# S5 layer with a top-4 mixture of experts on one core: another router order, S5 rotations on GpSimd, sums kept in PSUM, a ring of eleven pairs

## The chip, the core and the metric

The kernel runs on one core of a Trainium2 chip. The metric is the device time in microseconds (us) of one execution, from the first to the last instruction with what lies around them; lower is better. All data is float32.

## What is computed

One decoder layer for 256 tokens of width 1024 (the reference, cut to what the kernel does):

```python
proj = x @ w_in                                  # 1024 x (768 + 256)
y_mix = s5_mixer(proj[..., :768], ...)           # 48 groups x 64 complex states, scan over 256 tokens, gelu, gate
y_mem = memory_cross_attention(proj[..., 768:], mem_k, mem_v)   # 4 heads over 256 memory rows
y = concatenate([y_mix, y_mem]) @ w_out
h = layer_norm(ALPHA * x + y, ln1_g, ln1_b)
logits = h @ router_w + router_b                 # 32 experts
top_val, top_idx = top_k(logits, 4); gates = softmax(top_val)
gu = h[rows of expert e] @ w_gu[e] + b_gu[e]     # 1024 x 2048
a = clamped_swiglu(gu); y_e = a @ w_down[e] + b_down[e]         # 1024 x 1024
out = layer_norm(ALPHA * h + sum over experts of gate * y_e, ln2_g, ln2_b)
```

The weights of the 32 experts are 12.6 MB each and are all read, 403 MB of the 424.62 MB that the program moves.

## The kernel before

**Memory.** One SBUF tile `big` is cut into slots of 8 KB per partition (1 MB), 22 of them. A slot holds several tensors one after another; the table `slot_of` (L85 to L92) says which ("wsc" after "ptmp0" in slot 0, and so on). For the experts' weights the slots 0 to 19 are taken two at a time as blocks of 2 MB: `ring` (L99) lists ten pairs in the order in which they come free, and `next_block` (L101) takes the next one in rotation. An expert takes six blocks: four of `w_gu` (`load_gu`, L1128) and two of `w_down` (`load_down`, L1137). All these loads are issued by SP in program order; a load waits until its pair's last reader is done, and the next load waits behind it. At expert 18 one pair leaves the ring for constants of the end.

**Order.** `Ordered` (L127) and `pin` (L116) keep VectorE (V), ScalarE (S), SP and TensorE (through `mm` and `tr`, L141 to L145) in program order. GpSimd (G) isn't pinned, and VectorE isn't from L1165 on. PSUM has eight banks of 128x512, handed out by `bank` (L105) from one pool; a new bank waits for the release of an old one.

**S5 and attention (L157 to L882).** The projection runs on TensorE; the discretised S5 parameters and their powers `apw` are made by VectorE (L310 to L424). `power` (L467) multiplies the matrices B and C with the powers, 128x2048 at a time, on VectorE, and GpSimd adds the halves. `kb` (L553) makes the kernel taps `kr`, VectorE adds D (`dsk`) at L563, `kc` (L614) transposes them. Then VectorE makes the rotations' table `w_re`, `w_im` (L568 to L608, L662): three squarings `sq` of the angle (24 columns each), and `doubled`, which doubles the table from 1 to 32 columns; each complex product is six instructions (`cmul4`, L576). `rotated` (L729) applies them to the transposed state `sv`, scans it, and the output products `yb` follow. ScalarE in between copies `kc`, shifts, and copies transposes (`m1tp`, `sip`, `stp`).

**Gate and router.** After the memory half of W_out (`out_mem`, `yp`), TensorE transposes the gate's bias and gamma/beta (`bgp`, L856 to L861), makes the router's bias with beta folded in (`rbp`, L865) and multiplies the gate's weights (`zp`, L871). W_out's other 24 products (512 columns each) go into four banks `yp` (L930 to L937), one per token tile i and column half hf; VectorE adds the residual and takes the statistics of LayerNorm (L938, L939), GpSimd makes the reciprocal root. VectorE normalises x2 at once (L943) and GpSimd applies gamma and beta (`affine`, L917). `logits` (L964) transposes the normalised x2 of a tile (`hTp`), multiplies it with gamma-scaled router weights `wg` into 32 rows, copies, and `logits_t` turns them back; `chosen` (L984) takes the top 4 and a mask, `ranks` (L996) counts each token's place in its expert.

**Experts (L1250 to L1322).** `gather` (L1031) makes one-hot matrices `oh` and multiplies them with h (`xgp`): the tokens of two experts at once, 64 slots each. Per expert: `up` (L1064, banks `gu`), `act` (L1075, clamp and SwiGLU on VectorE and ScalarE), `act_t` (transposes `atp`), `up_bias` for the next expert, `down` (L1095, bank `dn`). After each pair `combine` (L1109) multiplies with the gates' transposes (`ogT`) into four banks `cb`, and VectorE adds them to `acc` in SBUF. At expert 30 `acc` is loaded into four banks `accp` by products with the identity, and the last sums go on there; `finish` (L1208) normalises and stores.

## Time and profile before

| | |
|---|---|
| runs | 1080.88, 1082.1, 1080.85 us; median 1080.88 |
| the profiled execution | 1082.37 us, its span 1080.7 us |
| TensorE (PE) busy | 1004.5 us, 93% of the span |
| VectorE (DVE), ScalarE (ACT), GpSimd (POOL) busy | 276.5, 152.1, 45.2 us |
| moved | 424.62 MB, mean 393 GB/s |
| TensorE's granted clock, mean | 0.994 of full speed |

The page of the profile divides the span into 40 equal slices and gives, for each, the busy tenths of every engine and the rate of the transfers. A group of instructions is named by line, engine, operation and tiles (out<-in); "L135" and "L142" are the lines of helpers, so groups are told apart by their tiles. TensorE's records come in passes: x16 for eight products. "Idle before <-releaser" is how long the engine stood before the instruction and what ended that.

### The profile page before, as it was taken

The numbers are of one execution on the slowest core, as the hardware profiler recorded it, in microseconds if no ns is written. First come the engines' busy times: TensorE is split into PE (matmuls) and PEld (weight loads), VectorE is DVE, ScalarE is ACT, GpSimd is POOL, SyncE is SP. The second block draws the span as 40 slices with busy tenths as digits, with TensorE's granted clock in tenths as the row PEclk, the third lists the DMA queues.
The fourth block names the chain that finished last, engine by engine and source line by source line (L and its number), as shares of the span: only waits on it lengthen the run. The fifth ranks groups of instructions, "written<-read, shape, count | busy, mean of one in ns | idle before, by whom it ended". The sixth has DMA issues, their size and how long they took to land.

```text
span 1080.7 us, 12435 instructions
## 1 busy us (share of the span) xinstructions
PE 1004.5 (93%) x5301; PEld 440.3 (41%) x5301; DVE 276.5 (26%) x627; ACT 152.1 (14%) x286; POOL 45.2 (4%) x57
## 2 busy tenths in 40 slices
PE   9998999999999999898989888899989999898994
PEld 8885554434343433243333232333433342323331
DVE  7993251121212221112121112102121211121013
ACT  3493020101010100010101010000101110100001
POOL 1800030000000000000000000000000000000001
PEclk9999999999999999999999999999999999999998
DMA  9959779999999999999999999999999999999992
GB/s 300 157 180 343 306 270 425 426 428 426 427 426 426 426 429 427 425 426 428 426 426 427 427 410 428 426 426 427 427 426 426 427 427 426 428 427 427 426 422 102
DMA packets 43843, 424.62 MB, mean 393 GB/s; under 512 B 11218, under 2 KB 14182, under 8 KB 19080
## 3 DMA queue, kind: packets, MB, share of 16 engines
q1 hardware_dynamic: 43288, 422.73, 95.3%
q10 hardware_dynamic: 496, 1.05, 0.3%
q8 instruction: 43, 0.70, 0.3%
q14 instruction: 16, 0.13, 0.0%
HBM read 421.93 MB, written 1.84 MB: 392 GB/s over the span
## 4 chain that ended last, share of the span: by engine, by line
DMA 53%; PE 37%; DVE 8%; issue 1%; ACT 0%; ACTq 0%; POOL 0%; DVEq 0%; SPq 0%
DMA big<-in_exp_w_gu_dram 46%; PE gu_e L142 14%; PE dn_e L142 7%; DMA big<-in_exp_w_down_dram 7%; DVE big L135 5%; PE xgp_e L142 3%; PE tail L142 3%; PE yp L142 3%; PE cb_e L142 2%; PE zp L142 1%; PE accp L142 1%; PE atp_e L145 1%; PE busy L142 1%; PE lgp L142 0%; PE yb L142 0%
## 5 line engine op out<-in xcount | busy, mean ns | idle before, releaser
L142 PE MATMUL gu_e<-big,xg_e 128*64 128x512 f32 x1984 | 442.9, 595 | 54.7 <-DMA big<-in_exp_w_gu_dram 54.0
L142 PEld LDWEIGHTS gu_e<-big,xg_e 128*64 128x64 f32 x1984 | 137.1, 137 | 354.6 <-issue 247.6
L142 PE MATMUL dn_e<-big,xl_te 128*64 128x512 f32 x960 | 212.6, 595 | 0.0
L1078 DVE TENSOR_SCALAR xl_e<-gu_e 128x512 f32<-128x512 f32 x31 | 21.4, 692 | 443.1 <-PE gu_e L142 443.1
L142 PEld LDWEIGHTS dn_e<-big,xl_te 128*64 128x64 f32 x960 | 66.3, 137 | 144.3 <-issue 119.9
L1105 DVE COPY y_e<-dn_e 64x512 f32<-64x512 f32 x30 | 20.5, 683 | 234.7 <-PE dn_e L142 234.7
L135 ACT ACTIVATE gu_e<-xl_e 128x512 f32<-128x512 f32 x31 | 18.6, 601 | 416.4 <-DVE xl_e L1078 416.4
L142 PE MATMUL xgp_e<-oh_e,big 128*128 128x128 f32 (+1 forms) x544 | 67.1, 282 | 0.0
L142 PEld LDWEIGHTS xgp_e<-oh_e,big 128*128 128x128 f32 x544 | 65.5, 196 | 0.1
L142 PE MATMUL cb_e<-y_e,ogT_e 128*128 128x512 f32 x112 | 52.1, 603 | 0.0
L135 ACT COPY y_e<-dn_e 64x512 f32<-64x512 f32 x30 | 17.4, 581 | 243.8 <-DVE y_e L1105 243.8
L148 DVE TENSOR_TENSOR big<-big,cb_e 128x512 f32<-128x512 f32 x52 | 33.5, 679 | 6.2 <-PE cb_e L142 6.1
L142 PE MATMUL gu_e<-bgu,ident 32*64 32x512 f32 x248 | 33.7, 612 | 0.0
L142 PEld LDWEIGHTS cb_e<-y_e,ogT_e 128*128 128x128 f32 x112 | 20.2, 189 | 30.3 <-issue 24.3
L135 DVE TENSOR_TENSOR big<-big 128x768 f32<-128x768 f32 (+10 forms) x35 | 25.4, 740 | 14.6 <-ACT big L135 14.1
L142 PE MATMUL yp<-big 128*128 128x512 f32 x64 | 28.2, 595 | 0.0
L135 DVE TENSOR_TENSOR big<-big,tab 128x2048 f32<-128x2048 f32 x12 | 26.6, 2276 | 0.2 <-DVE big L135 0.2
L148 POOL TENSOR_TENSOR big<-big 128x512 f32<-128x512 f32 (+1 forms) x10 | 26.1, 2632 | 2.7 <-DVE big L135 1.9
L135 ACT COPY xg_e<-xgp_e 128x512 f32<-128x512 f32 x32 | 18.7, 585 | 48.3 <-PE xgp_e L142 48.3
L135 ACT COPY xl_te<-atp_e 128x512 f32<-128x512 f32 x30 | 17.6, 585 | 52.7 <-PE atp_e L145 46.0
L1080 DVE TENSOR_SCALAR xr_e<-gu_e 128x512 f32<-128x512 f32 x31 | 21.4, 691 | 2.9 <-PE gu_e L142 0.2
L1081 DVE SCALAR_TENSOR_TENSOR xr_e<-xr_e,xl_e 128x512 f32<-128x512 f32 x32 | 22.0, 688 | 0.5
(282 smaller groups left out, 578.3 us busy)
## 6 DMA issues: line engine op xcount, KB each, us to landing
big<-in_exp_w_gu_dram SPq DMA_DIRECT2D x128, 2048.0 KB, 38.1
big<-in_exp_w_down_dram SPq DMA_DIRECT2D x62, 2048.0 KB, 39.1
big<-in_l_w_in_dram SPq DMA_DIRECT2D x3, 1024.0 KB
big<-in_w_out_dram SPq DMA_DIRECT2D x3, 1024.0 KB
big<-in_exp_w_down_dram SPq DMA_DIRECT2D x3, 1024.0 KB
big<-in_x_dram SPq DMA_DIRECT2D x3, 512.0 KB
big<-in_l_s_w_glu_dram SPq DMA_DIRECT2D x2, 768.0 KB
big<-in_l_w_in_dram SPq DMA_DIRECT2D x2, 512.0 KB
```

Of the source, the lines that this page charges most:

```text
L135: return lambda *a, **k: pin(f(*a, **k))
L142: pin(PE.matmul(o, lhsT, rhs, start=start, stop=stop, skip_group_check=shared))
L145: pin(PE.transpose(o, in_, ident if idn is None else idn))
L148: return (eng or V).tensor_tensor(out=o, in0=x0, in1=x1, op=op)
L1078: V.tensor_scalar(out=xl_, in0=ps[0], scalar1=7.0, scalar2=None, op0=ALU.min)
L1080: V.tensor_scalar(out=xr, in0=ps[1], scalar1=7.0, scalar2=-7.0, op0=ALU.min, op1=ALU.max)
L1081: V.scalar_tensor_tensor(out=xr, in0=xr, scalar=1.0, in1=xl_, op0=ALU.add, op1=ALU.mult)
L1105: eng(y[:, 512 * dh : 512 * dh + 512], ps[dh][64 * dh : 64 * dh + 64, :])
```

## The change

- `big` gets a 23rd slot, the ring an eleventh pair; tensors change their slots, and the pairs' order is new. `apw`, its scratch and `r8` move into a slot. `bgu` is held as four quarters of 512 columns, in four loads.
- S5: the three squarings, the first four columns of the table (`w4`) and the squares up to the fourth power's are made on GpSimd right after `r8`; VectorE doubles from 4 on. D is added by three TensorE products into the banks of `kb`.
- The transposes of biases and gamma/beta and the folded router bias (now spread to all partitions) are made after the first `kps`, copied by ScalarE; `wg` on GpSimd earlier; the column sums of `wg` give a correction `lfix`.
- Router: logits come from x2 before normalisation, token by row, and are corrected with mean and reciprocal root (`fixed`); h is made by VectorE in two steps (`first`, `second`), and the order of the stages is written out.
- Experts: `combine` sums into four banks `accp` from the first pair on; `gather_pair` fills its banks one after the other and comes before the gates' transposes; `y` has one buffer.

```diff
...
-NBIG = 22
+NBIG = 23
...
-        "mem_sb tz1 gb", "wk wgl1", "x_sb m1p1 wgl2", "xT prob yT", "rawb m1p2 wo0", "rawc m1p0 wo1", "win_2 wo3",
-        "win_3 wgl0", "win_0 sv wo2", "win_1 tz2 ymT", "wv h_sb", "ut kr pT x2 acc",
+        "mem_sb tz1 gb", "ut kr pT x2", "x_sb m1p1 wgl2", "xT prob", "rawb m1p2 wo0", "rawc m1p0 wo1", "win_2 wo3",
+        "win_3 wgl0", "win_0 sv wo2", "win_1 tz2 ymT", "wk wgl1", "pow yT", "wv h_sb",
...
-    ring = [2 * k + n for k in (0, 1, 2, 3, 4, 6, 8, 7, 9, 5) for n in range(0, 2, ROWS)]
+    ring = [2 * k + n for k in (0, 1, 2, 3, 4, 8, 6, 10, 7, 9, 5) for n in range(0, 2, ROWS)]
...
-    bgu = keep_t("bgu", (2 * NE, D))
-    for b in range(2):
-        SP.dma_start(bgu[NE * b : NE * b + NE, :], b_gu[0, :, D * b : D * b + D])
+    bgu = keep_t("bgu", (P, 512))
+    for q in range(4):
+        SP.dma_start(bgu[NE * q : NE * q + NE, :], b_gu[0, :, 512 * q : 512 * q + 512])
...
-    apw = small("apw", (P, 2, Q + 1, NG))
-    t1, t2 = small("t1", (P, 4, NG)), small("t2", (P, 4, NG))
+    pw = big_tile("pow")
+    apw = pw[:, 0:864].rearrange("p (q k g) -> p q k g", q=2, g=NG)
+    t1, t2 = (pw[:, 864 + 192 * n : 1056 + 192 * n].rearrange("p (k g) -> p k g", g=NG) for n in range(2))
...
     for _ in range(3):
         tt(mv_, mv_, mv_, ALU.mult, G)
-    r8 = small("r8", (P, 24, NC))
+    r8 = pw[:, 1248:2016].rearrange("p (r c) -> p r c", c=NC)
     G.tensor_copy(r8, mv_.unsqueeze(2).to_broadcast([P, 24, NC]))
     G.memset(r8[:, :, 0], 0.0)
+
+    def cmul4(o_re, o_im, x_re, x_im, y_re, y_im, t, eng=None):
+        yield tt(t[0], x_re, y_re, ALU.mult, eng)
+        yield tt(t[1], x_im, y_im, ALU.mult, eng)
+        yield tt(t[2], x_re, y_im, ALU.mult, eng)
+        yield tt(t[3], x_im, y_re, ALU.mult, eng)
+        yield tt(o_re, t[0], t[1], ALU.subtract, eng)
+        yield tt(o_im, t[2], t[3], ALU.add, eng)
+
+    def sq(o, i_, t, eng=None):
+        return cmul4(o[:, 0], o[:, 1], i_[:, 0], i_[:, 1], i_[:, 0], i_[:, 1], t, eng)
+
+    e_, f_, w4, s4g = small("e_", (P, 2, 24)), small("f_", (P, 2, 24)), small("w4", (P, 2, 24, 4)), small("s4g", (P, 4, 24, 2))
+    s4q = [s4g[:, n, :, 0] for n in range(4)]
+    G.memset(w4[:, 0, :, 0], 1.0)
+    G.memset(w4[:, 1, :, 0], 0.0)
+    for o, i_ in ((e_, cv), (f_, e_), (e_, f_)):
+        together(sq(o, i_, s4q, G))
+    G.tensor_copy(w4[:, :, :, 1], e_)
+    together(sq(f_, e_, s4q, G))
+    together(cmul4(
+        w4[:, 0, :, 2:4], w4[:, 1, :, 2:4], w4[:, 0, :, 0:2], w4[:, 1, :, 0:2],
+        *(f_[:, q].unsqueeze(2).to_broadcast([P, 24, 2]) for q in range(2)), [s4g[:, n] for n in range(4)], G,
+    ))
+    together(sq(e_, f_, s4q, G))
 
     tab = [bank("tab0")[:, 0 : (Q + 1) * NG], bank("tab1")[:, 0 : (Q + 1) * NG]]
     S.copy(tab[0], apw[:, 0].rearrange("p k g -> p (k g)"))
@@ -559,8 +585,9 @@
                     ps[32 * j : 32 * j + 32, P * l : P * l + P], ca_pad[:, NH * g : NH * g + 2 * NH], m1p[g],
                     l == 0, True, True,
...
-    tt(kr[:, :, NH : 2 * NH], kr[:, :, NH : 2 * NH], dsk, ALU.add)
+        pv_ = ps.rearrange("p (l n) -> p l n", l=4)
+        mm(pv_[:, :, 0:NH], ident, dsk[:, 4 * b : 4 * b + 4, :], False, True, True)
+        S.copy(kr[:, 4 * b : 4 * b + 4, NH:144], pv_)
...
+    for q, w_ in enumerate((wre, wim)):
+        G.tensor_copy(w_[:, :, 0:4], w4[:, q])
...
-    for o, i_ in ((e_, cv), (f_, e_), (e_, f_)):
-        together(sq(o, i_))
-    G.memset(wre[:, :, 0], 1.0)
-    G.memset(wim[:, :, 0], 0.0)
-    w_state = [1, e_, f_]
+    w_state = [4, e_, f_]
...
+                    wre[:, :, n : 2 * n], wim[:, :, n : 2 * n], *((w4[:, 0], w4[:, 1]) if n == 4 else (wre[:, :, 0:n], wim[:, :, 0:n])),
+                    b_[0], b_[1], [u[:, :, 0:n] for u in us],
                 ),
-                sq(nxt, cur) if 2 * n < NC else iter(()),
+                sq(nxt, cur, s4) if 2 * n < NC else iter(()),
...
+    bgp = bank("bgp")
+    tr(bgp[:, 0:6], bg6, ident[0:6, 0:6])
+    tr(bgp[:, 8:24], gl16, ident[0:16, 0:16])
+    bglu, gcol = small("bglu", (P, 6)), small("gcol", (P, 16))
+    S.copy(gcol, bgp[:, 8:24])
+    S.copy(bglu, bgp[:, 0:6])
+    wg, wgs, lfix = keep_t("wg", (P, KT, NE)), small("wgs", (P, NE)), keep_t("lfix", (P, 2, NE))
+    rbp = bank("rbp")
+    for kt in range(KT):
+        mm(rbp[:, 0:NE], gcol[:, KT + kt : KT + kt + 1].to_broadcast([P, P]), wr[:, kt, :], kt == 0, False)
+    mm(rbp[:, 0:NE], ones[0:1, :], rb, False, True)
+    S.copy(lfix[:, 1], rbp[:, 0:NE])
...
+    tt(wg, wr, gcol[:, 0:KT].unsqueeze(2).to_broadcast([P, KT, NE]), ALU.mult, G)
...
-    bgp = bank("bgp")
...
-    tt(wg, wr, gcol[:, 0:KT].unsqueeze(2).to_broadcast([P, KT, NE]), ALU.mult, G)
-    rbp = bank("rbp")
-    for kt in range(KT):
-        mm(rbp[0:1, 0:NE], gcol[:, KT + kt : KT + kt + 1], wr[:, kt, :], kt == 0, False)
-    mm(rbp[0:1, 0:NE], ones[0:1, 0:1], rb, False, True)
-    V.tensor_copy(rb2, rbp[0:1, 0:NE])
+    V.tensor_reduce(out=wgs, in_=wg.rearrange("p k e -> p e k"), axis=AX.X, op=ALU.add)
...
+    wsp = bank("wsp")
+    mm(wsp[:, 0:NE], ones, wgs, True, True)
+    S.mul(lfix[:, 0], wsp[:, 0:NE], -1.0)
...
-        n = 2 if tag in ("ogT", "y") else 1
+        n = 2 if tag == "ogT" else 1
...
+    mean, rs = [None] * 2, [None] * 2
+    lgp = bank("lgp")
+
+    def added(i, hf):
+
+        hs = slice(512 * hf, 512 * hf + 512)
+        out_q(i, hf, range(QO, 8))
+        stt(x2[:, i, hs], x2[:, i, hs], ALPHA, yp[i][hf], ALU.mult, ALU.add)
+        norm_stats(x2[:, i, hs], hf, f"{i}")
+
+    def turned(i, hf):
+        ps = bank(f"hTp{i}{hf}")
+        for k in range(4):
+            kt = 4 * hf + k
+            tr(ps[:, P * k : P * k + P], x2[:, i, kt * P : (kt + 1) * P])
+        S.copy(hT[i][:, 4 * hf : 4 * hf + 4, :], ps.rearrange("p (k n) -> p k n", k=4))
+
+    def logits(i, hf):
+        for kt in range(4 * hf, 4 * hf + 4):
+            mm(lgp[:, NE * i : NE * i + NE], hT[i][:, kt, :], wg[:, kt, :], kt == 0, kt == KT - 1, True)
+
+    def normed(i):
+        mean[i], rs[i] = norm_of_stats(f"{i}")
+
+    def first(i, hf):
+        hs = slice(512 * hf, 512 * hf + 512)
+        stt(h_sb[:, i, hs], x2[:, i, hs], mean[i], gb[:, 0, hs], ALU.subtract, ALU.mult)
+
+    def second(i, hf):
+        hs = slice(512 * hf, 512 * hf + 512)
+        stt(h_sb[:, i, hs], h_sb[:, i, hs], rs[i], gb[:, 1, hs], ALU.mult, ALU.add)
+
+    def fixed(i):
+
+        stt(lg[:, i, :], lfix[:, 0], mean[i], lgp[:, NE * i : NE * i + NE], ALU.mult, ALU.add)
+        stt(lg[:, i, :], lg[:, i, :], rs[i], lfix[:, 1], ALU.mult, ALU.add)
+
+    def chosen(i):
...
-                    ps[b][64 * hf : 64 * hf + 64, :], sel[b],
-                    bgu[NE * b : NE * b + NE, 512 * hf : 512 * hf + 512], True, False, True,
+                    ps[b][64 * hf : 64 * hf + 64, :], sel[2 * b + hf],
+                    bgu[NE * (2 * b + hf) : NE * (2 * b + hf) + NE, :], True, False, True,
...
+    added(0, 0)
+    added(0, 1)
+    turned(0, 0)
+    normed(0)
+    first(0, 0)
+    first(0, 1)
+    added(1, 0)
+    turned(0, 1)
+    logits(0, 0)
+    logits(0, 1)
+    fixed(0)
+    second(0, 0)
+    chosen(0)
+    second(0, 1)
+    rkp0, rkp1 = bank("rkp0"), bank("rkp1")
+    added(1, 1)
+    turned(1, 0)
+    mm(rkp0[:, 0:NE], lower, msk[:, 0, :], True, True)
+    turned(1, 1)
+    normed(1)
+    ranks(0, rkp0[:, 0:NE])
+    logits(1, 0)
+    logits(1, 1)
+    mm(rkp1[:, 0:NE], ones, msk[:, 0, :], True, False, True)
     ps = up_bias("e0", sel_of(0))
-    lg0 = logits_t(0, lg0)
-    lg1 = logits(1)
...
-    lg1 = logits_t(1, lg1)
-    mm(rkp1[:, 0:NE], ones, msk[:, 0, :], True, False, True)
+    oh_e0 = wt((P, 2, 2 * CAP), "oh", "e0")
+    ts(oh_e0[:, 0, 0:CAP], iota64, rk[:, 0, 0:1], ALU.is_equal)
+    first(1, 0)
+    first(1, 1)
+    fixed(1)
+    chosen(1)
...
+    def gather_pair(n, xg, ranks):
+
+        oh = wt((P, 2, 2 * CAP), "oh", n)
+        for i in range(2):
+            for k, rank in enumerate(ranks):
+                ts(oh[:, i, CAP * k : CAP * k + CAP], iota64, rank[i], ALU.is_equal)
+        for k4 in range(2):
+            ps = bank(f"xgp{k4}_{n}")
+            for i in range(2):
+                for kt in range(4 * k4, 4 * k4 + 4):
+                    mm(
+                        ps[:, P * (kt % 4) : P * (kt % 4) + P], hv[:, i, kt // ROWS, kt % ROWS], oh[:, i, :],
+                        kt % 4 == 0 and i == 0, i == 1, True,
+                    )
+            S.copy(xg[:, 4 * k4 : 4 * k4 + 4, :], ps.rearrange("p (k c) -> p k c", k=4))
...
+    accp = []
+
+    def combine(y, ogT, late=None, stop=False):
+
+        if not accp:
+            alpha_id = wt((P, P), "xl", "alpha")
+            V.tensor_scalar(out=alpha_id, in0=ident, scalar1=ALPHA, scalar2=None, op0=ALU.mult)
+            for i in range(2):
+                accp.append([bank(f"accp{i}{hf}") for hf in range(2)])
+                for hf in range(2):
+                    mm(accp[i][hf], alpha_id, h_sb[:, i, 512 * hf : 512 * hf + 512], True, False)
+        for i in range(2):
+            for dh in range(2):
+                ds_ = slice(512 * dh, 512 * dh + 512)
+                mm(accp[i][dh], ogT[:, i, :], y[:, ds_], False, stop)
+                if late is not None:
+                    mm(accp[i][dh], late[:, D + P * i : D + P * i + P], late[:, ds_], False, False)
+
+    def combine_on(n, y, ogT, acc):
         for i in range(2):
             for dh in range(2):
                 ps = bank(f"cb{i}{dh}_{n}")
                 ds_ = slice(512 * dh, 512 * dh + 512)
-                mm(ps, ogT[:, i, :], y[:, ds_], True, late is None)
-                if late is not None:
-                    mm(ps, late[:, D + P * i : D + P * i + P], late[:, ds_], False, True)
-                if first:
-                    a = stt(acc[:, i, ds_], h_sb[:, i, ds_], ALPHA, ps, ALU.mult, ALU.add)
-                else:
-                    a = tt(acc[:, i, ds_], acc[:, i, ds_], ps, ALU.add)
-                last_of["acc"] = a.ins.name
+                mm(ps, ogT[:, i, :], y[:, ds_], True, True)
+                tt(acc[:, i, ds_], acc[:, i, ds_], ps, ALU.add)
...
     def rest_of_ranks():
-        chosen(1, lg1)
         mm(rkp1[:, 0:NE], lower, msk[:, 1, :], False, True, True)
+        second(1, 0)
         ranks(1, rkp1[:, 0:NE])
-        busy(3)
+        busy(2)
 
     xgs = wt((P, KT, 2 * CAP), "xg", "e0")
-    gather("e0", xgs[:, :, 0:CAP], [ranks_of(0)], iota64, rest_of_ranks)
-    V = nc.vector
+    gather("e0", xgs[:, :, 0:CAP], [ranks_of(0)], iota64, rest_of_ranks, lambda: second(1, 1), oh_e0)
...
+    V = nc.vector
...
-            accp = [[bank(f"accp{i}{hf}") for hf in range(2)] for i in range(2)]
             a = act(f"e{e}", ps)
+            combine(*last)
             y = wt((P, D), "y", f"e{e}")
-            for i in range(2):
-                for hf in range(2):
-                    ds_ = slice(512 * hf, 512 * hf + 512)
-                    mm(accp[i][hf], ident, acc[:, i, ds_], True, False)
-                    mm(accp[i][hf], last[2][:, i, :], last[1][:, ds_], False, False)
...
-        if e % 2 == 0:
-            y = wt((P, D), "y", f"e{e}")
         if last is not None:
             combine(*last, late if e == NE - 12 else None)
             last = None
+        if e % 2 == 0:
+            y = wt((P, D), "y", f"e{e}")
         if e % 2:
+            xgs = wt((P, KT, 2 * CAP), "xg", f"e{e + 1}")
+            gather_pair(f"e{e + 1}", xgs, [ranks_of(e + 1), ranks_of(e + 2)])
             ogT = gates_t(f"e{e}", og, P)
             og = wt((P, 2, 2 * CAP), "og", f"e{e + 1}")
-            xgs = wt((P, KT, 2 * CAP), "xg", f"e{e + 1}")
-            gather(f"e{e + 1}", xgs, [ranks_of(e + 1), ranks_of(e + 2)], iota64)
...
+    slot_of["acc"] = ring.pop(0)
+    acc = big_tile("acc").rearrange("p (i d) -> p i d", i=2)
...
```

## Rows read from the trace of the kernel before

**Rows 1.** The page's second part, bytes moved in 40 equal slices of the span.

```profile
GB/s 300 157 180 343 306 270 425 426 428 426 427 426 426 426 429 427 425 426 428 426 426 427 427 410 428 426 426 427 427 426 426 427 427 426 428 427 427 426 422 102
```

**Rows 2.** TensorE timeline, 500-565 us: start, us, engine line op out<-in xcount [idle <-releaser].

```profile
512.32 3.65 PE L142 MATMUL gu_e<-big,xg_e 128*64 128x512 f32 x16 [1.25 <-DMA big<-in_exp_w_gu_dram]
517.22 3.65 PE L142 MATMUL gu_e<-big,xg_e 128*64 128x512 f32 x16 [1.25 <-DMA big<-in_exp_w_gu_dram]
```

**Rows 3.** Chain of waits, `up` of experts 1 and 3: start us, us, what.

```profile
181.18 13.73 PE gu_e L142 x64
...
233.42 13.73 PE gu_e L142 x64
```

**Rows 4.** Timeline of TensorE, 117 to 156 us (router, first gather, first `up`).

```profile
139.92 1.04 PE L145 MATMUL hTp<-ident,big 128*128 128x128 f32 x8
...
148.88 2.08 PE L142 MATMUL xgp_e<-oh_e,big 128*128 128x64 f32 x16
...
154.55 1.94 PE L142 MATMUL gu_e<-big,xg_e 128*64 128x512 f32 x8 [0.68 <-ACT xg_e L135]
```

**Rows 5.** Chain of waits, from the last `up` with a wait to the tail.

```profile
1021.89 3.65 PE gu_e L142 x16
1025.54 7.06 PE accp L142 x16
...
1048.35 7.04 PE tail L142 x32
```

**Rows 6.** Timeline of SP's queue, 122 to 170 us (issues of expert weights).

```profile
138.40 10.29 SPq L135 DMA_DIRECT2D big<-in_exp_w_gu_dram  x3
...
158.25 3.76 SPq L135 DMA_DIRECT2D big<-in_exp_w_down_dram  x2
```

**Rows 7.** Windows of 3 us: length, busy (x) by engine, PEclk, DMA share, GB/s.

```profile
135.00:138.00 3.00, 3.00 (x8) 1.33 (x7) 2.29 (x5) 0.00 (x0) 2.10 (x3) 1.00 0.00 0
159.00:162.00 3.00, 3.00 (x18) 1.00 (x16) 0.00 (x0) 0.00 (x0) 0.00 (x0) 1.00 0.98 295
```

**Rows 8.** Timeline of VectorE, 14 to 59 us (sine series, first squaring).

```profile
14.90 0.44 DVE L135 SCALAR_TENSOR_TENSOR sn<-sn,r 128x48 f32<-128x48 f32 x2
...
57.99 0.45 DVE L135 TENSOR_TENSOR s<-cv 128x24 f32<-128x24 f32 x4
```

**Rows 9.** Timeline of ScalarE, 49 to 75 us.

```profile
52.16 2.50 ACT L135 COPY big<-kc 128x256 f32<-128x256 f32 x6 [2.40 <-PE kc L145]
...
69.86 1.83 ACT L135 COPY big<-stp 128x512 f32<-128x512 f32 x4
```

**Rows 10.** Chain of waits, 71 to 140 us.

```profile
71.84 1.70 DVE big L135 x2
...
98.20 3.44 PE yp L142 x8
...
103.40 15.89 PE zp L142 x96
119.29 20.80 PE yp L142 x48
```

**Rows 11.** Timeline of TensorE, 42 to 60 us.

```profile
51.41 2.84 PE L145 MATMUL kc<-ident,big 128*128 128x128 f32 x24 [2.06 <-DVE big L135]
```

**Rows 12.** Timeline of GpSimd, 12 to 40 us.

```profile
14.99 0.83 POOL L148 TENSOR_TENSOR mv__402<-mv__402 128x24 f32<-128x24 f32 x3
...
30.30 0.59 POOL L148 TENSOR_TENSOR dsk<-dsk,same 128x192 f32<-128x192 f32 x1 [12.48 <-DMA dsk<-in_l_s_d_dram]
```

**Rows 13.** Timeline of VectorE, 139 to 152 us (router of the second token tile).

```profile
140.12 0.69 DVE L135 SCALAR_TENSOR_TENSOR big<-big,yp 128x512 f32<-128x512 f32 x1 [2.02 <-PE yp L142]
...
145.12 1.01 DVE L148 TENSOR_TENSOR ex<-m 128x4 f32<-128x4 f32 x1
...
148.96 0.20 DVE L135 MAX8 m<-lg 128x8 f32<-128x32 f32 x1
...
150.02 0.37 DVE L135 TENSOR_REDUCE msk<-xr_og 128x32 f32<-128x128 f32 x1
```

More of the change, by code (lines that the diff above doesn't have):

```diff
@@ L1039, in gather @@
             for k, rank in enumerate(ranks):
-                ts(oh[:, i, CAP * k : CAP * k + CAP], base, rank[i], ALU.is_equal)
+                if i or first_too:
+                    ts(oh[:, i, CAP * k : CAP * k + CAP], base, rank[i], ALU.is_equal)
+            if i:
+                after()
             for kt in range(KT):
@@ L1322 @@
         if e % 2:
-            last = (f"e{e}", y, ogT)
+            last = (y, ogT)
     finish(
```

98 lines of the change are left out of this document (13 added, 85 removed).

## Prediction

> **What bounds the kernel now.** I read the page's slices first. From the seventh of the 40 on, the core moves 425 to 429 GB/s in nearly every slice; the first six hold 157 to 343 [rows 1]. So the time is the moment from which the weight stream never stops, plus the bytes then left, plus a tail; what matters is what delays that moment.
>
> The timeline of TensorE in mid-stream shows who waits: each block of gate and up weights (2 MB) makes TensorE stand 1.25 us, and the blocks come 4.90 us apart [rows 2]. An expert is six blocks, 29.4 us of transfer. In the early experts TensorE has the data and needs 52.24 us from one `up` to the second after it, 26.1 us per expert [rows 3]. From the first `up` to the end of expert 30's the mean is (1025.54 - 13.73 - 154.55) / 30 = 28.6 us [rows 3, 4, 5], so TensorE has about 2.5 us per expert to lose before it is the bound.
>
> Then SP's issues and the three-microsecond windows. Ten blocks fit the ring before expert 0 is consumed. Blocks 8 to 10 go out from 138.40 us, when W_out's last products release their slots; block 11 goes out at 158.25 us, 3.70 us after `up` of expert 0 began and had used up the first block [rows 4, 6]. Between 135 and 138 us nothing moves, and between 159 and 162 us only 295 of some 425 GB/s, so block 11 flows from 159.9 us, 1.65 us after its issue [rows 7]. From there the stream is whole: block 12 starts at 159.9 + 4.9 = 164.8 us.
>
> **The S5 stage.** Forty-two small complex-product instructions leave VectorE (three squarings, the doublings from 1 and 2 with their squarings); at 0.45 / 4 = 0.11 us [rows 8] that is 4.6 us, and the add of D, some 0.5 us, goes too. I cost this gain at nothing: the rotations need S5's transposed state, whose ScalarE copies end at 69.86 + 1.83 = 71.69 us, and the first rotation starts at 71.84 us [rows 9, 10]. ScalarE is busy in one run back to the `kc` copies at 52.16 us, so VectorE will only arrive early and stand.
>
> What sets the stage is when `kc` starts. Today TensorE ends `kps` at 49.35 us and waits 2.06 us for VectorE's add of D [rows 11]. That wait goes, but new work stands in its place: three products with D at 0.26 us (2.08 / 8, the gather's 128x128 by 64 [rows 4]) ahead of `kps`, then two transposes at 0.13 us (1.04 / 8 [rows 4]), a small ScalarE copy of some 0.4 us with its handovers, and nine router products, whose stationary operand is now 128 columns wide, again at 0.26 us. That makes 49.35 + 0.8 + 0.3 + 0.4 + 2.3 = 53.1 us, 1.7 us later than 51.41 us. After the 0.15 us that the rotations had in hand, **plus 1.5 us**. Below, the nine cost a transpose's 0.13 us each: plus 0.4. A gain is excluded, since no operation before `kc` gets shorter. Above, GpSimd holds VectorE back somewhat: plus 3.5, half of the rival below. I take 0.26, the row with the same width of stationary operand.
>
> GpSimd gets 36 of those products between its last preparation and 30.30 us, where it stood idle for 12.48 us; at 0.83 / 3 = 0.28 us they fill 10 us of it [rows 12]. Behind them on its queue are the multiplication for D and the sums of the first matrices, which TensorE needs at 43 us; by these prices they start as before. Where the gap is too short, what is late next is `kb`. SP's queue gets two issues more, the bias table in four loads instead of two, ahead of the load of `wv`, which is read some 40 us later: nothing.
>
> A page of the Trainium skill speaks against this part: SBUF — State Buffer, section "SBUF: two separate sides", says that VectorE and GpSimd share one port pair under an exclusive lock, so a VectorE instruction with two SBUF inputs blocks for the whole of a GpSimd one. One row fits it: a four-element product took 1.01 us beside a GpSimd product, where one of 24 elements takes 0.11 us alone [rows 8, 13]. By that rule alone the sum would come out as the second rival's.
>
> **From the gate to the first expert.** The transposes of the biases, the folded router bias and their copies leave the gap between `yp` and `zp`: 103.40 - (98.20 + 3.44) = 1.76 us [rows 10]. One product of ones with the weight sums comes before `yp` instead, 0.3 us with its start: **minus 1.5**, within 0.2.
>
> In the router I walked the new order from the first `yp` on (119.29 us now, 35.3 us ahead of the first `up` at 154.55 us [rows 4, 10]). The 24 products take 20.8 us as now, but four half-transposes of token tile 0 (0.52 us each pair of four, two such) and eight logit products (0.26 us) stand inside them, 3.1 us, so the last quarter is summed at 23.9. VectorE adds and takes statistics: 0.69 + 0.69 + 0.21 + 0.15 with gaps, 2.0 [rows 13]: 25.9. Then rank, one-hot, two halves of `first` at 0.7: 27.7. Two corrections of the logits at 0.2: 28.2. Top-4 and mask as now from 148.96 to 150.39 us, 1.4 [rows 13]: 29.6. The count product queues behind the first half of the gather, which TensorE ends at about 30.8, and with rank and one-hot that gives 31.7. The second half of the gather 2.08 and the copy 0.7 [rows 4]: 34.5. **Minus 0.8**; with the last halves of `second` uncovered plus 1, with logit products at 0.13 us minus 2.
>
> So `up` of expert 0 starts at 154.55 + 1.5 - 1.5 - 0.8 = 153.75 us.
>
> **The eleventh pair.** Blocks 6 to 8 can go at the end of the gate, 9 and 10 when the last W_out products end (22 to 24 us after the first, about 141 and 143 us), 11 when `second` of the last quarter ends (32.4 after it, about 151.7 us). They land by 158.1 us. Block 12 needs expert 0's first block to be used: 153.75 + 3.70 + 1.65 = 159.1 us. Against 164.8 us that is 5.7 us, of which 0.8 is counted above: **minus 4.9**. Bounds: minus 4.9 and nothing.
>
> **The experts.** The sum in four PSUM banks takes 52 VectorE adds away, which TensorE doesn't wait for: nothing. The gather of a pair now precedes the gates' transposes; the same work, and ScalarE's copy of the activations comes some 0.4 us later in odd experts. At expert 2, TensorE waits about 2 us for a scaled identity, which takes the buffer of the activation and so stands behind it on VectorE (the first sum and the activation's transposes queue behind that wait), and does four more products, 3.5 us by half of the tail's eight [rows 5]. Slack covers both: nothing. Without it they would cost 0.2 us per expert and 5.5 us once.
>
> **The tail.** Four products that reload the sum are gone, half of 7.06 us [rows 5]. But the last block of expert 30's down weights lands six blocks after 1021.89 us, at 1051.3 us; half of `down`, 3.5 us, follows, to 1054.8, where now it ends at 1055.39 [rows 5]. **Minus 0.5**; bounds minus 3 and nothing.
>
> Sum: -0.8 - 4.9 - 0.5 = -6.2 us. The profiled execution took 1082.37 us (its span 1080.7 and 1.7 around it), so 1076.2; it stands 1.5 us above the median of the three runs, 1080.88, which gives **1074.7 us**. All starts shift alike, so sizes within the head only move this number.
>
> **The rivals.** First, the eleventh pair buys nothing: its block is released so late, by `second` or by the queue in front of it on SP, that block 12 starts no sooner than by the earlier `up`. For it: the slots with gamma and x2 are the last released. Against: 158.1 is before 159.1. Then 1079.6 us. Chance 0.11.
>
> Second, GpSimd blocks VectorE in the S5 preparation. From 30.30 - 12.48 = 17.82 us on [rows 12] VectorE has some 27 products of two SBUF operands before the big ones with the power tables; if each waits for one GpSimd product of 0.28 us, 7.5 us come before everything: 1082.2 us. For it the 1.01 us row [rows 13]; against it, beside three GpSimd products at 14.99 us [rows 12] two steps of VectorE's sine series took 0.44 us together [rows 8], not a GpSimd product more each. Chance 0.08.
>
> Third, the slower side: with four banks left, `up`, gather, gate and activation transposes, the next bias products and `down` wait for each other's evictions. The point that decides is 2.5 us per expert. At 3.0 us an expert takes 29.1 us, 30 times 0.5 above today's mean, 16 us, less 0.8 and less the 3.5 us of the tail: 1093 us. Against it: an eviction takes 1.83 / 4 = 0.46 us on ScalarE [rows 9], and five of them in a row are 2.3 us. Chance 0.06.
>
> Fourth, better: router products at 0.13 us and the tail's 3.5 us partly kept; S5 plus 0.4, router minus 1.5, tail minus 1.5: minus 8.9 us, 1072 us. Chance 0.17. My forecast has 0.58.
>
> **How the numbers follow.** A measurement here can tell 0.2%, 2.2 us, from no change. Forecast (its own range 1071.5 to 1078) and fourth rival are faster, 0.75; the first and the larger part of the second lie within it, 0.17; the third and the rest are slower, 0.08. The range from 1070.5 to 1080.5 takes in the bounds of the S5 stage, the router and the tail, and the first rival.
>
> **What would show it.** Right: `kc` about 1.7 us later, the rotations waiting for ScalarE, `up` of expert 0 near 153.8 us, block 12 issued near 157.5 us, a dead stretch of the queue still ahead of W_out's end, and VectorE idle in the experts. Wrong: full GB/s from the same time as before (first rival), VectorE's products after 17.8 us stretched (second), TensorE waiting for ACT or DVE between `up` and `down` by over 2.5 us (third).

## The result, and the profile after

The changed kernel takes 1072.99 us (median of ten executions, 1071.89 to 1079.34); the kernel before took 1080.89 us (median of ten). The ratio of the means is 0.994, with a 95% interval of 0.9928 to 0.9953; by the medians it is faster by 7.9 us, where 6.2 us were forecast. Seven of ten executions lie between 1071.9 and 1073.5 us, three near 1079 us with a lower mean granted clock of TensorE (0.987 instead of 0.995); the experiments come back to these.

The page of the profiled execution (1072.42 us, span 1070.6 us) shows where the stream of weights begins to be whole; against [rows 1] the fifth and sixth slices hold 424 and 314 GB/s instead of 306 and 270:

```profile
GB/s 303 166 151 329 424 314 429 428 417 430 427 428 427 425 429 428 426 430 427 428 426 429 429 409 428 429 428 427 427 427 428 427 428 427 427 428 428 429 422 98
```

TensorE's timeline, with the columns of [rows 4], gives the milestones of the head: `kb`, with which the S5 stage begins (the products with D, second row, stand between its parts), the router's bias ahead of `kc`, the transposes `stp` of S5's state, the products `yb` that wait for the scan, the gate's sum of weights, the first `yp` behind it, the two halves of the first gather, and `up` of expert 0; further down the scaled identity and the tail.

```profile
41.91 1.32 PE L142 MATMUL kb<-big 128*32 128x128 f32 x32
43.16 0.43 PE L142 MATMUL kb<-dsk,ident 128*128 128x64 f32 x2
...
50.40 1.97 PE L142 MATMUL rbp<-wr,gcol 128*128 128x32 f32 x16 [0.31 <-ACT gcol L135]
...
52.63 2.84 PE L145 MATMUL kc<-ident,big 128*128 128x128 f32 x24
...
70.40 1.84 PE L145 MATMUL stp<-ident,big 128*128 128x128 f32 x12
...
88.04 0.42 PE L142 MATMUL yb<-big 128*32 128x128 f32 x8 [0.97 <-DVE big L135]
88.91 2.61 PE L142 MATMUL yb<-big 128*32 128x128 f32 x88 [0.44 <-DVE big L135]
...
115.95 0.41 PE L142 MATMUL wsp<-wgs,ones 128*128 128x32 f32 x2
116.19 13.98 PE L142 MATMUL yp<-big 128*128 128x512 f32 x32
...
144.11 2.10 PE L142 MATMUL xgp_e<-oh_e,big 128*128 128x64 f32 x16
...
146.97 2.10 PE L142 MATMUL xgp_e<-oh_e,big 128*128 128x64 f32 x16
149.80 7.52 PE L142 MATMUL gu_e<-big,xg_e 128*64 128x512 f32 x34 [0.73 <-ACT xg_e L135]
...
219.04 5.40 PE L142 MATMUL accp<-big,xl_alpha 128*128 128x512 f32 x8 [2.45 <-DVE xl_alpha L1163]
...
1042.06 3.65 PE L142 MATMUL tail<-big 128*64 128x512 f32 x16 [1.14 <-DMA big<-in_exp_w_down_dram]
```

VectorE's timeline: the powers in S5's preparation, the big products behind them, the first rotation, and the mask of the second token tile. GpSimd's, below it, holds some of what moved there, and the last row is ScalarE's, the four copies of the transposed state.

```profile
17.86 5.19 DVE L135 TENSOR_TENSOR big<-big 128x48 f32<-128x48 f32 x18
...
26.26 4.49 DVE L135 TENSOR_TENSOR big<-big,tab 128x2048 f32<-128x2048 f32 x2 [0.19 <-DVE big L135]
...
72.02 2.88 DVE L135 TENSOR_TENSOR big<-big 128x768 f32<-128x768 f32 x3 [4.15 <-PE stp L145]
...
144.94 0.37 DVE L135 TENSOR_REDUCE msk<-xr_og 128x32 f32<-128x128 f32 x1
```

```profile
17.27 0.80 POOL L148 TENSOR_TENSOR s4g<-cv 128x24 f32<-128x24 f32 x4
...
23.10 1.17 POOL L148 TENSOR_TENSOR f__414<-s4g 128x24 f32<-128x24 f32 x2
...
27.88 0.45 POOL L148 TENSOR_TENSOR e__413<-s4g 128x24 f32<-128x24 f32 x2
```

```profile
71.09 1.83 ACT L135 COPY big<-stp 128x512 f32<-128x512 f32 x4
```

SP's queue, to hold against [rows 6]: block 11 is the first of the two at 147.64 us, ahead of `up`, and block 12 the second, 153.5 us, 3.7 us after `up` began.

```profile
147.64 6.18 SPq L135 DMA_DIRECT2D big<-in_exp_w_down_dram  x2
```

And its windows of 3 us, as in [rows 7]: the stretch without transfers ahead of W_out's end is still there, the dent behind the first `up` is small.

```profile
135.00:138.00 3.00, 3.00 (x16) 2.04 (x16) 2.02 (x7) 0.10 (x1) 0.00 (x0) 1.00 0.03 11
...
153.00:156.00 3.00, 3.00 (x18) 1.00 (x14) 0.99 (x5) 0.00 (x0) 0.00 (x0) 1.00 0.97 371
```

**Reading the two profiles together.** Three stretches are compared, from milestones of the timelines: `kb` to the first rotation (the S5 stage), rotation to the first `up`, first `up` to the end of the span. What lies ahead of `kb` is the arrival of x and W_in; it moved by up to 7 us between executions (41.9 to 49.2 us) and is no part of the change. All kernels of the study stand here, each by its profiled execution:

| kernel | `kb` to rotation | rotation to `up` | `up` to end |
|---|---|---|---|
| before | 28.97 | 82.71 | 926.15 |
| after | 30.11 | 77.78 | 920.8 |
| e1_again, e9_after_there (after) | 31.51, 31.57 | 77.79, 77.80 | 921.15, 921.02 |
| e2_ten_pairs | 31.70 | 77.78 | 926.21 |
| e3_alpha_late | 29.86 | 77.78 | 920.54 |
| e4_rot_dve | 29.87 | 77.79 | 920.44 |
| e5_alpha_twice | 31.53 | 82.02 | 924.97 |
| e6_rbp_gate | 26.91 | 80.78 | 920.23 |
| e7_sbuf_sum | 29.86 | 77.79 | 925.67 |
| e8, e11 (late gap, twice) | 27.25, 27.71 | 78.33, 78.30 | 920.10, 920.61 |
| e10_gap_only | 27.71 | 78.31 | 919.78 |
| e12_small_more | 27.25 | 87.67 | 919.97 |

Between the profiled executions of before and after, the span fell by 10.1 us: 0.96 by the earlier arrival (`kb` at 42.87 and 41.91 us), plus 1.14 in S5, minus 4.93 to the first `up`, minus 5.35 from there on. Part of the 4.93 was the bad luck of one execution: before, TensorE stood 1.85 us ahead of `yb`, and its granted clock fell to the lower level for these products, 4.28 us instead of 2.61 us. The timeline (with `stp`, which is wanted further down) and the windows (TensorE's columns alone) of before:

```profile
69.17 1.84 PE L145 MATMUL stp<-ident,big 128*128 128x128 f32 x12
...
87.67 0.43 PE L142 MATMUL yb<-big 128*32 128x128 f32 x8 [1.85 <-DVE big L135]
88.54 4.28 PE L142 MATMUL yb<-big 128*32 128x128 f32 x88 [0.44 <-DVE big L135]
```

```profile
90.00:92.00 2.00, 2.00 (x44) 0.50 0.89 287
```

Without that and the arrival, the two profiles differ by 7.5 us, near the medians' 7.9.

### The profile page after: what moved, and what is told of

Read it like the earlier page. It is cut to its first block, busy times and chain, and to the rows that moved or that the text cites. A ratio compares the mean times of both kernels' runs of the same rounds, so it can differ in the third digit from the quotient of the medians.

```text
span 1070.6 us, 12357 instructions
## 1 busy us (share of the span) xinstructions
PE 1003.3 (94%) x5297; PEld 442.6 (41%) x5297; DVE 245.6 (23%) x531; ACT 150.4 (14%) x288; POOL 49.2 (5%) x90
## 4 chain that ended last, share of the span: by engine, by line
PE 50%; DMA 45%; DVE 2%; ACT 1%; issue 0%; SPq 0%; ACTq 0%; POOL 0%; DVEq 0%; POOLq 0%
DMA big<-in_exp_w_gu_dram 29%; PE gu_e L142 20%; PE dn_e L142 11%; DMA big<-in_exp_w_down_dram 11%; PE xgp_e L142 4%; DMA big<-in_exp_b_down_dram 4%; PE accp L142 3%; PE yp L142 3%; DVE big L135 2%; PE ups L142 1%; PE zp L142 1%; DMA big<-in_l_w_in_dram 1%; PE tail L142 1%; ACT big L135 1%; PE atp_e L145 1%; PE qps L142 1%
## 5 line engine op out<-in xcount | busy, mean ns | idle before, releaser
L142 PE MATMUL accp<-y_e,ogT_e 128*128 128x512 f32 x128 | 59.4, 603 | 0.8 <-DVE y_e L1155 0.8
L142 PEld LDWEIGHTS accp<-y_e,ogT_e 128*128 128x128 f32 x128 | 23.2, 190 | 35.3 <-issue 33.7
L135 DVE TENSOR_TENSOR big<-big 128x96 f32<-128x96 f32 (+8 forms) x47 | 29.0, 635 | 21.1 <-ACT big L135 16.2
L1131 DVE TENSOR_TENSOR xr_e<-xr_e,gu_e 128x512 f32<-128x512 f32 x31 | 21.3, 687 | 6.4 <-ACT gu_e L135 3.3
```

What stands on the lines that cost most here:

```text
L135: return lambda *a, **k: pin(f(*a, **k))
L142: pin(PE.matmul(o, lhsT, rhs, start=start, stop=stop, skip_group_check=shared))
L1131: a = V.tensor_tensor(out=xr, in0=xr, in1=sg, op=ALU.mult)
```

## The experiments

Each kernel is the kernel after with the edit shown. The times come from three chips, each with the kernel before run beside them: e1 to e4 (before: 1082.25 us), e5 to e8 (1081.59) and e9 to e12 (1081.35). The ratios are to the kernel before on the same chip. Parts of a kernel are compared by the table above.

**e1_again and e9_after_there: the kernel after, unchanged**

> The changed kernel itself once more, to hold the others against. Theory: most executions near 1072.5 us and some near 1079 us, as 3 of the 10 so far. Theory for these: the 2.45 us wait for the scaled identity at expert 2 lets TensorE's granted clock fall, in those executions for longer than the 6 us of the profiled one, and the ring has only about 1 us to spare there, so that the next blocks are issued some 6 us late. Rival: the clock falls elsewhere, ahead of the first expert, and everything behind it shifts; then a profile of such an execution shows the first `up` late instead.

> The kernel after, unchanged, beside the next three on one chip. Every theory: undisturbed executions at 1071.7 to 1073.5, about one in five near 1079 with a mean clock of 0.987.

Measured: 1075.15 us (ratio 0.9938, 0.9921 to 0.9955) and 1073.77 us (0.9943, 0.9924 to 0.9962). With the first ten, 7 of 26 executions of the kernel after lie at 1078.9 to 1079.4 us with a mean clock of 0.986 or 0.987. Both profiled executions lost some 1.7 us in S5 (31.5 us from `kb` to the rotation, 29.87 where the clock held), by a fall of the granted clock just where the transposes of the biases and the bias products of 128x32 had run; windows of 2 us in e9_after_there, TensorE alone:

```profile
52.00:54.00 2.00, 2.00 (x17) 0.97 1.03 398
54.00:56.00 2.00, 2.00 (x12) 0.50 0.86 342
```

TensorE was busy in both windows (2.00 of 2.00); its last wait, 0.31 us ahead of the bias products, was over 3 us before the fall. The `kc` transposes, 2.84 us in the kernel after, took 4.50 us here. Four of the eight profiled executions with the bias products ahead of `kc` show this fall; none of the five without them there does, which with such counts can still be chance.

**e2_ten_pairs: the ring without the eleventh pair**

```diff
-    ring = [2 * k + n for k in (0, 1, 2, 3, 4, 8, 6, 10, 7, 9, 5) for n in range(0, 2, ROWS)]
+    ring = [2 * k + n for k in (0, 1, 2, 3, 4, 8, 6, 7, 9, 5) for n in range(0, 2, ROWS)]
```

> The eleventh pair is left out of the ring, all else as in the changed kernel. Theory (a block more before expert 0 is worth its 4.9 us): first `up` unchanged at 149.8 us, the block that reuses the first pair issued at 153.5 us, the end 4 to 5 us later, 1076.5 to 1077.4 us. Since a block more of PE's lag is then covered at expert 2, no executions near 1079 + 4.9 us. Rival (the pair buys nothing, the whole gain is the earlier first `up`): 1072.5 us.

Measured: 1077.88 us (0.9959, 0.9947 to 0.9972), 2.7 us above e1_again by medians, 4.8 us by the fastest executions (1076.79 and 1071.96). The two profiles are nearly the same as far as the first `up` (152.09 and 152.15 us), and the rest is 926.21 against 921.15 us: the pair is worth 5.06 us (the same stretch lies between 919.78 and 921.15 us in the profiled executions of the kernels with eleven pairs, e5_alpha_twice aside). SP's queue shows how: block 11 must wait for `up` (152.09 + 3.69), as before the change.

```profile
155.78 3.76 SPq L135 DMA_DIRECT2D big<-in_exp_w_down_dram  x2
```

**e3_alpha_late: the scaled identity and its four products at expert 20 instead of expert 2**

```diff
-        if not accp:
-            alpha_id = wt((P, P), "xl", "alpha")
...
+        if late is not None:
+            alpha_id = late[:, D + NT : D + NT + P]
...
-                mm(accp[i][dh], ogT[:, i, :], y[:, ds_], False, stop)
+                mm(accp[i][dh], ogT[:, i, :], y[:, ds_], opens, stop)
```

> The scaled identity and its four products with h move from the first sum (expert 2) to the sum at expert 20, where TensorE waits for weights. Theory: no wait and no fall of the granted clock at 216 to 224 us, SP's issue of block 28 some 4 us earlier, 0.7 us off most executions (1071.8 us) and none near 1079 us. Rival (the slower executions come from elsewhere): the same 3 in 10 stay, and the others are within 0.3 us of the changed kernel.

Measured: 1073.06 us (0.9914, 0.9901 to 0.9926). The wait of 2.45 us and the four products are gone from expert 2, but from the first `up` to the end it takes 920.54 us, where the kernel after took 920.8, 921.15 and 921.02. At expert 2 the change costs a few tenths at most; e6_rbp_gate and e10_gap_only, which keep it there, took 920.23 and 919.78 us. So the 0.7 us of the theory are not seen. The median is 2.1 us below e1_again, but the profiled executions are equal (1074.94 and 1075.0 us): here `kb` came 2.2 us later and the S5 stage, with no fall of the clock, was 1.65 us shorter. None of the five executions is near 1079 us.

**e4_rot_dve: S5's squarings and first doublings on VectorE again, at their old place**

```diff
-        together(sq(o, i_, s4q, G))
+        together(sq(o, i_, s4q))
```

> The squarings and the first four columns of the rotations' table go back to VectorE at their old place; all else as in the changed kernel. Theory (VectorE then stands 4.15 us for the transposed state, so its relief is hidden): 36 small instructions, 3.8 us, fill that wait; 1072.4 to 1073 us. Rival (the relief is where the time before the first expert came from): 1076 us.

Measured: 1072.79 us (0.9932, 0.9911 to 0.9953). VectorE now finishes just in time for the first rotation, and nothing moves (29.87 us from `kb`, as in e3_alpha_late and e7_sbuf_sum):

```profile
72.17 2.88 DVE L135 TENSOR_TENSOR big<-big 128x768 f32<-128x768 f32 x3 [0.29 <-PE stp L145]
```

Of VectorE's standing time, 4.15 us in the kernel after, 0.29 is left; the instructions put back took it from 58.22 to 62.44 us. As long as the bias block stands ahead of `kc`, the move to GpSimd is worth nothing. One of the six executions took 1080.28 us, at a mean clock of 0.987.

**e5_alpha_twice: the four products at expert 2 done twice**

```diff
-            V.tensor_scalar(out=alpha_id, in0=ident, scalar1=ALPHA, scalar2=None, op0=ALU.mult)
+            V.tensor_scalar(out=alpha_id, in0=ident, scalar1=ALPHA / 2, scalar2=None, op0=ALU.mult)
...
-                    mm(accp[i][hf], alpha_id, h_sb[:, i, 512 * hf : 512 * hf + 512], True, False)
+                    for n in range(2):
+                        mm(accp[i][hf], alpha_id, h_sb[:, i, 512 * hf : 512 * hf + 512], n == 0, False)
```

> The kernel after, with the scaled identity made of half of ALPHA and its four products at expert 2 done twice (eight products; the output is the same). Theory: at expert 2 the ring has no spare time, so four more products of 128x512 (0.9 us each at the full clock) delay the next block's load by 3.6 us and the stream never gets that back: the time from the first up to the end grows by 3.6 us, the median to about 1077 where the kernel after gives 1073 to 1075; the load that follows expert 2 is issued 3.6 us later, and the weights' rate falls in the slices behind it. Rival (my prediction's words, slack covers both): within 0.5 us of the kernel after.

Measured: 1077.67 us, scattered from 1073.51 to 1089.47 (0.9961, 0.9944 to 0.9978). The theory holds roughly: the eight products took 8.83 us where four took 5.40, and from `up` on the profiled execution took 924.97 us, some 4 us more than the kernel after; by the fastest executions, 1073.5 against 1071.7, it is 1.8 us. So expert 2 had room for the wait and four products, and little beyond. The size stays open between the two. The profiled execution was disturbed elsewhere too and took 1089.47 us: `kb` came at 49.18 us, and the granted clock fell in the router. This is the only trace of a fall of that kind in a kernel with the router unchanged (windows of 2 us, TensorE alone):

```profile
150.00:152.00 2.00, 2.00 (x21) 0.98 0.99 426
152.00:154.00 2.00, 2.00 (x10) 0.50 1.00 426
...
164.00:166.00 2.00, 2.00 (x8) 0.60 0.82 352
```

Nearly 14 us at half the clock lower the mean over the span by 6.8 / 1088 = 0.006, most of the step from 0.995 to 0.987. In time, the first `up` came 4.24 us later by the table; that the part of the half clock behind it cost anything is not shown (in e12_small_more it reaches as far behind `up`, and the rest takes 919.97 us). So this trace accounts for 4.24 of the 6 to 7 us between the two groups of executions. That gave the question for e12_small_more.

**e6_rbp_gate: the bias block back at its old place in the gate**

```diff
-    bgp = bank("bgp")
-    tr(bgp[:, 0:6], bg6, ident[0:6, 0:6])
...
-    S.copy(lfix[:, 1], rbp[:, 0:NE])
...
     out_mem(0)
+    bgp = bank("bgp")
+    tr(bgp[:, 0:6], bg6, ident[0:6, 0:6])
...
+    S.copy(lfix[:, 1], rbp[:, 0:NE])
```

> The kernel after, with the transposes and the products of the router's bias and the wg product moved back to their old place behind out_mem(0), in the gate. Theory (the trace of the kernel after): the S5 stage gives back little, since the first rotation came only 0.2 us later (first rotation 0.2 to 0.4 us earlier than in the kernel after, kc about 2.5 us earlier), while the gate gets its gap of 1.8 us and the products of 2 us back: first up 1.5 to 3.5 us later, median 2 to 3 us above the kernel after. Rival (my prediction's term of +1.5 us for S5): kc earlier pulls everything behind it 1.5 us forward, so that the move is worth under 1 us in all.

Measured: 1073.31 us (0.994, 0.9919 to 0.9961). The theory fell: the S5 stage gave back 3.2 us (30.11 to 26.91), the gate took 3.0 (77.78 to 80.78), in all nothing, as the rival had it (under 1 us in all). I had compared absolute times, in which the earlier arrival of the inputs hid a later rotation. VectorE's first rotation, with what it still waits:

```profile
69.69 2.88 DVE L135 TENSOR_TENSOR big<-big 128x768 f32<-128x768 f32 x3 [1.73 <-PE stp L145]
```

VectorE stood idle for 1.73 us ahead of it; the work that went to GpSimd, some 4.1 us by e4_rot_dve, would not have fitted. So here GpSimd's part does pay, about 4.1 - 1.7 = 2.4 us by this estimate (the two edits together were not run). Two of the seven executions lie at 1078.87 and 1079.17 us with a mean clock of 0.987, without the bias block ahead of `kc`.

**e7_sbuf_sum: ten pairs, and the experts' sum in SBUF as before**

```diff
-                mm(accp[i][dh], ogT[:, i, :], y[:, ds_], False, stop)
+                mm(ps, ogT[:, i, :], y[:, ds_], True, late is None)
...
+                    tt(acc[:, i, ds_], acc[:, i, ds_], ps, ALU.add)
```

> Ten pairs of slots, and the experts' sum kept in SBUF as in the kernel before (four products into fresh banks per pair of experts and four VectorE additions, the sum preloaded into the last banks with the plain identity). Theory: VectorE's 52 additions wait for nothing that TensorE needs, so the time is that of the kernel with ten pairs and the sum in PSUM (1077.9 on the last chip, 5 us above the kernel with eleven) within 1 us: the four banks are worth nothing by themselves, they only free the slot. Rival: the additions and the missing scaled identity matter: 2 us or more apart from the ten-pair kernel, in one direction or the other.

Measured: 1078.3 us (0.9982, 0.9969 to 0.9996). With the 52 additions back on VectorE (33.5 us of work) it takes 925.67 us from the first `up` on, against 926.21 with the sum in the banks. By medians it is 1078.3 against 1077.88 us on another chip, by the fastest executions 1077.99 against 1076.79. So the four banks by themselves are worth about a microsecond at most, and nothing from the first `up` on in the profiles; their gain is the slot.

**e8_late_gap and e11_late_gap_again: e3's edit, and the bias products behind `pv`, where TensorE waits for VectorE**

```diff
     S.copy(ymem, pv.rearrange("p (q n) -> p q n", q=2))
+    rbp = bank("rbp")
+    for kt in range(KT):
+        mm(rbp[:, 0:NE], gcol[:, KT + kt : KT + kt + 1].to_broadcast([P, P]), wr[:, kt, :], kt == 0, False)
...
+    S.copy(lfix[:, 1], rbp[:, 0:NE])
```

> Two edits on the kernel after: the scaled identity and its products moved to expert 20 (as in e3_alpha_late), and the seventeen products' block of the router's bias moved from ahead of kc to behind the context product pv, where TensorE stands about 1 us for VectorE. Theory: kc comes 2 us earlier but the first rotation only 0.2 us; the gap takes 1 of the block's 2 us, so first up moves by -0.2 to +1 us; the end is that of e3_alpha_late (about 0.6 us below the kernel after from the first up on), and no execution comes near 1079. Rival: the early kc brings the scan and the states forward by 1.5 us, and first up comes 1 us or more earlier: median 1072 or below.

> The kernel of e8_late_gap again, on the chip of the kernel after: 1070 to 1071, 2 to 3 us below the kernel after; if the executions near 1079 come from expert 2, none is among its executions, if they come from the router, about one in five or six is 6 to 7 us longer.

Measured: 1070.08 us (0.9895, 0.9881 to 0.991) and 1070.44 us (0.9897, 0.9883 to 0.9912). The rival of the first text was right. TensorE's timeline of e8_late_gap:

```profile
42.82 1.08 PE L142 MATMUL kb<-big 128*32 128x128 f32 x32
...
50.68 2.84 PE L145 MATMUL kc<-ident,big 128*128 128x128 f32 x24
...
85.04 1.97 PE L142 MATMUL rbp<-wr,gcol 128*128 128x32 f32 x16
86.94 0.40 PE L142 MATMUL rbp<-rb,ones 1*128 1x32 f32 x2
87.28 2.83 PE L142 MATMUL yb<-big 128*32 128x128 f32 x96
...
148.40 8.80 PE L142 MATMUL gu_e<-big,xg_e 128*64 128x512 f32 x40 [0.73 <-ACT xg_e L135]
```

`kc` starts 7.86 us after `kb` instead of 10.72, the rotation 2.4 to 2.9 us earlier in e11 and e8 (counted from `kb`), and behind `pv` the block costs only 0.5 us, since it fills the waits ahead of `yb` (0.97 and 0.44 us in the kernel after). None of the eight executions is above 1071.03 us.

**e10_gap_only: the block behind `pv`, the scaled identity at expert 2**

The second edit of e8_late_gap alone.

> The kernel after with one edit: the router bias's block of products moved from ahead of kc to behind pv; the scaled identity stays at expert 2. Theory (from e6 and e8: the block ahead of kc costs the S5 chain 3 us, and the gap behind pv takes 1 of them): first up 2 us earlier counted from the kb products than in the kernel after, median 1.5 to 2.5 us below it; late scaled identity and late block together give 1070.1, so the block alone gives 1070.5. Rival (the identity's wait at expert 2 is worth the difference): median within 0.7 us of the kernel after.

Measured: 1070.94 us (0.9917, 0.99 to 0.9933), 2.8 us below e9_after_there on the same chip and 0.5 us above e11_late_gap_again. The move of the block is the part that pays: 1.9 us from `kb` to the first `up` by the table, and 1.9 us by the fastest executions (1069.76 and 1071.66 us). The medians differ by more since three of the ten executions of e9_after_there lie near 1079 us and none of the six here.

**e12_small_more: e8_late_gap with sixteen more small products in the router**

```diff
     logits(1, 1)
+    fill = bank("fill")
+    for _ in range(16):
+        mm(fill[:, 0:NE], ones, ones[:, 0:NE], True, True)
```

> The kernel of e8_late_gap with sixteen more products of 128x32 (ones by ones into a spare bank, 0.24 us each, 3.9 us) behind the second tile's logits. It tells where the executions near 1079 come from; its base has no scaled identity at expert 2. Theory (e5's trace: the granted clock fell to 0.50 at 152 us behind the router's stretch of small products and stayed there for 14 us, 6.9 us of work): undisturbed executions at 1074, but the fall now comes in most executions, which then take 1079 to 1082 at a mean clock near 0.988, and the trace shows the granted clock at 0.50 from the gather of expert 0 on. Rival (the falls come from expert 2 or from the start): all executions at 1073 to 1075 and a granted clock of 1.00 in the router.

Measured: 1081.08 us (0.9995, 0.9987 to 1.0004), 10.6 us above e11_late_gap_again for 3.9 us of work. All eleven executions have a mean clock of 0.986 to 0.988. The clock falls where the theory put it, with TensorE busy (windows of 2 us, TensorE alone, then its timeline):

```profile
142.00:144.00 2.00, 2.00 (x20) 0.96 1.07 459
144.00:146.00 2.00, 2.00 (x11) 0.50 0.96 401
```

```profile
141.65 5.01 PE L142 MATMUL fill<-ones 128*128 128x32 f32 x32
...
158.03 7.22 PE L142 MATMUL gu_e<-big,xg_e 128*64 128x512 f32 x26 [0.73 <-ACT xg_e L135]
```

From rotation to `up` it takes 87.67 us, 9.34 more than in e8_late_gap: 3.9 of work, the rest, 5.4 us, the clock; by the medians it is 10.6 - 3.9 = 6.7 us. A run of small products in the router is thus enough to bring a fall of this size. That the executions of the kernel after near 1079 us are the same fall is supported by the mean clock, by the size as far as it goes (4.2 us in e5's trace, 5.4 to 6.7 here, 6 to 7 to be explained) and by e5's trace, not shown in a trace of that kernel. The theory of e1_again, a longer fall at expert 2, is not excluded: none of the 13 executions of e3, e8 and e11, which have no scaled identity there, is near 1079 us. But neither is one of the six of e10, which have it, and e7, which has none, shows 1083.81 us at a mean clock of 0.989 once in eight.

## Why the prediction was right, point by point

**The eleventh pair and the tail** (minus 4.9 and minus 0.5): 5.35 us between before and after from the first `up` on, 5.06 by e2_ten_pairs, where 5.4 were forecast. The working held: block 11 goes out ahead of `up`, block 12 took over its wait 3.7 us into `up`. As the sum had it, the tail waits for data, 1.14 us ahead of the last half of expert 30's `down` (1042.06 us); e7_sbuf_sum, where the reload of the sum is back, is no slower than e2_ten_pairs, so the four products saved were worth nothing or nearly nothing there.

**The S5 stage** (plus 1.5): plus 1.14 us from `kb` to the rotation in this execution, 0.9 in the others that kept the full clock. The sum was near, one step in it failed: "I cost this gain at nothing: the rotations need S5's transposed state, whose ScalarE copies end at" 71.69 us. The first product of `rotated` reads only one half of that state (`s_re`), the first two of the four copies. In the kernel after the rotation starts at 72.02 us, while the copies run from 71.09 to 72.92 us: 1.62 us behind the start of the `stp` transposes (70.40 us), before 2.67 us (69.17 and 71.84 us, [rows 10]). So it does not wait for the last copy. Before, VectorE itself was the last to be ready, by 1.0 us; two ends 0.15 us apart had been read as a wait, and VectorE's relief was worth this 1.0 us. Against this, `kc` came 1.9 to 2.2 us later instead of 1.7. That the sum came out near is in part luck: the two errors have opposite signs.

**The gate** (minus 1.5): the gap of 1.76 us is gone, and the sum of the weights takes 0.24 us from its start to the first `yp`: minus 1.5.

**The router** (minus 0.8): this is the term of the sum that was mis-sized. From the first `yp` to the first `up` it takes 149.80 - 116.19 = 33.6 us, 1.7 less than before. Counted from the first `yp`, the mask of the second tile ended at 145.31 - 116.19 = 29.1 us, where the walk had 29.6; the first half of the gather at 30.0, not 30.8; so the count product behind it, and with it the second half, started at 30.8, not 31.7. The order of the walk was right, nearly each step of it a little too long: 0.3 us by the last quarter of W_out, 0.5 by the mask, 0.9 by the second half. No run takes the router's order back alone; the 1.7 us are read from the timelines, where this stretch takes 33.6 us in every profiled execution whose clock held there and whose router is the same.

**A clock fall that was not read.** Before's profiled execution had lost 1.67 us in `yb`. It is 1.5 us above its median, and I subtracted that at the end without asking for its place; it cancels in the medians, so it did no harm.

**The experts** (nothing): right. The additions on VectorE were not waited for (e7_sbuf_sum). "Slack covers both" held for expert 2 within a few tenths (e3_alpha_late), with little margin left (e5_alpha_twice).

**The rivals.** The first fell with e2_ten_pairs. The second, GpSimd blocking VectorE, fell by its size. The start of VectorE's eighteen products and of the big ones behind them, before:

```profile
18.38 0.32 DVE L135 TENSOR_TENSOR t<-apw 128x48 f32<-128x48 f32 x2
...
26.28 4.48 DVE L135 TENSOR_TENSOR big<-big,tab 128x2048 f32<-128x2048 f32 x2 [0.19 <-DVE big L135]
```

From the one to the other it took 7.90 us before and 8.40 us after (17.86 to 26.26), and 7.91 us again in e4_rot_dve, where GpSimd has none of these products (the eighteen took 4.78 us there, 5.19 in the kernel after). So GpSimd held VectorE up by 0.5 us, not by 7.5, and an earlier start hid it. The rule of the Trainium skill that spoke for it (SBUF — State Buffer, section "SBUF: two separate sides", an exclusive lock on the shared ports) does not give the time here, if VectorE stands for one GpSimd product each time. What did stretch was GpSimd: two products of 24 columns took 1.17 us beside VectorE's products of 768 columns (23.10 us), and 0.45 us beside the big ones (27.88 us), whose `tab` lies in PSUM.

The third fell: between an expert's `up` and its `down` TensorE waits for another engine only once before the tail, the 2.45 us at expert 2, and in the tail for 1.33 us, as before the change. Between the forecast and the fourth, the result is nearer to the fourth, by the router.

## What to carry to other kernels

Count a stage from its own first instruction, not from the start of the span: the arrival of the inputs moved by more than any term here, and absolute times made the bias block ahead of `kc` look like 0.2 us when it cost 3. A block of products moved out of one gap and ahead of another chain only changes the place of its price (e6_rbp_gate); where TensorE waits anyway, behind `pv`, the same block's products brought 1.9 us up to the first `up`. Work taken off an engine that waits is worth what it frees for others: VectorE's additions freed a slot for the ring, which was all of the 5 us.
